# A two-layer diffusion step: the columns of shift and scale, the first value products and the first output products in another order

## The chip, the cores and the metric

The kernel runs on one core of a Trainium2 chip. The metric is the device time of one execution in microseconds (us), taken as the median of several runs. The core has five engines, each with its own queue, worked off in order: PE (TensorE, matrix products; its weight loads are listed as PEld), DVE (VectorE), ACT (ScalarE), POOL (GpSimd) and SP (SyncE, which issues most DMA transfers). ACT issues transfers too, in the same queue as its computation.

## The reference

One inference step with two layers over 512 latent tokens and 128 context tokens, 1024 channels wide. Layer 0 mixes tokens by neighbourhood attention, layer 1 by grouped attention; behind each mixer stands a gated feed-forward part (FFN) with a convolution of width 3. Before each part the tokens are normed and get a scale and a shift that are computed from a conditioning vector:

```python
sh_ap, sc_ap, g_ap, ... = adaln(c_ctx, ada_w[l], ada_b[l])      # silu(c) @ w + b, in six pieces
hs = rmsnorm(xs, norm_mix_pre[l]) * (1.0 + sc_as) + sh_as
qs, ks_, vs = na_qkv(hs, na_w_qkv[i])                            # h @ w_qkv
os_ = neighbourhood_attention(qs, ks_, vs, ...)                  # softmax over near keys and all context keys
xs = xs + g_as * rmsnorm(os_ @ w_o, norm_mix_post[l])
```

The change is within layer 0's mixer: from the first loads to the products with `w_o`.

## The kernel before, in words

A product of two fp32 matrices is made of three passes with rounded operands (`passes`, L176): high part by high part, high by low, low by high. So each weight tile of 128x1024 numbers (512 KB) is loaded as `wr`, cast by ACT to its high part `wh` (L165), and DVE or POOL subtracts to get the low part `wl` (L167, `wsplit`). The same is done for activations: `hT` is a pair of tensors with the channels on the partitions (eight blocks k = 0 to 7 of 128 channels) and the 640 tokens in the columns.

**The start** (L483 to L632). Five token tiles `x_0` to `x_4` are loaded, normed (`x_norm`) and turned by PE (`x_turn`, `tr`) into `xT`. The scale and shift of the first layer come in four groups of 256 channels each. For a group, `mod_load` loads four tiles `wf` of `ada_w`, `mod_rows` makes a `row` of 16 products, ACT copies it to `rs`, and `mod_cols` turns it by four products `col` into columns `gcol` and `hcol` for two blocks k. With these ACT makes the high part of `hT` (L568), and DVE scales `xT` (L569) and makes the low part (L570). The first 256 of 1024 value columns are then made: `v_part(i, cs)` adds, for the token tiles in `cs`, the products `vp` of the blocks 2i and 2i + 1, 15 for a block over all five tiles. These products of group i need the columns of group i and the value weights `wv`, loaded in two tiles of four blocks each.

**The heads** (from L740). Sixteen heads in eight pairs. A generator `stream` yields one step after the other of the remaining products: queries and keys of a pair (`qk`, six products a step) and values (`vp`). `fill()` runs one step. Ahead of head 0, `PRO` steps are run. For each head, `scores` of four slots make products `s`, DVE adds a bias table `tb` and finds the minimum `nm`, ACT makes exponentials `p`, POOL scales them (L918); `turns` 0 to 2 turn them by PE (`tp`), and `values` multiplies pairs of heads with the values (`po`). A list of words sets the order on PE: `ORDER` for heads 0 to 12, `ORDER2` from 13, in two variants for even and odd heads. `f` is a step of the stream, `s0` to `s3` are scores of the next head, `t0` to `t2` turns of this head, `v` the values of the last two heads. In heads 1, 5, 9 and 13, `p0` makes the context tokens' own scores (`sp`, POOL's scaling at L658), `p1` turns them (`tp<-ident,pp`), `p2` multiplies them with the values. The bias table of a head is built by POOL from three loads `tr` that ACT issues (L870), into one buffer for all heads.

When the stream has ended, the products with `w_o` (`y`, `part0(t, p)`: three products of 512 columns for token tile t and pair p) take its place: the generator `early`, started behind head 12. They need the split outputs `oh` and `ol` of the pair (`o_split`, L960 and L961) and split weights.

PE's order is fixed as written: each PE instruction is tied to the one before. On the other engines a scheduler sets the order.

Of the kernel before, what the change touches and what calls it, by code (L numbers as in the profile page):

```python
# [2 lines left out]

# [15 lines left out]
P = 128  # L19
# [82 lines left out]
def hybrid_step(ctx: ExitStack, tc: tile.TileContext, A, O):  # L102
# [16 lines left out]
    def f32(t):  # L119
        return t.bitcast(F32)  # L120
# [17 lines left out]
    nc.sync.dma_start(cc[0:8, :], A["c"].rearrange("o (k p) -> (o k) p", p=P))  # L138
    nc.sync.dma_start(cc[8:16, :], A["c_ctx"].rearrange("(k p) -> k p", p=P))
    nc.sync.dma_start(cc[16:32, :], A["ada_b"][0, 0:2048].rearrange("(k p) -> k p", p=P))  # L140
    nc.sync.dma_start(cc[32:40, :], A["norm_mix_pre"][0].rearrange("(k p) -> k p", p=P))
    nc.sync.dma_start(ident, A["k_ident"])
# [17 lines left out]
    def wsplit(src, a, b, low=None, own=None, pin=False):  # L160
# [4 lines left out]
        i = nc.scalar.copy(hi, raw)  # L165
        lo = q.tile([P, a, b], F32R, tag="wl", name="wl")
        j = (low or nc.vector).tensor_sub(lo, raw, f32(hi))  # L167
        if pin:
            tc.keep_in_program_order(i)
            tc.keep_in_program_order(j)  # L170
        return hi, lo
# [307 lines left out]
    vts_of = {}  # L479
    with ExitStack() as s:  # L480
        sp = s.enter_context(pool("st"))
        sel = sp.tile([P, 2], F32, name="sel")
        nc.vector.tensor_reduce(sel, ident.rearrange("p (j q) -> p q j", q=32)[:, 0:2, :], axis=AX.X, op=ALU.add)  # L483
# [9 lines left out]

        ct = bk.get("ct")
# [55 lines left out]
        def mod_cols(i, rs):  # L550
# [14 lines left out]
            for k in (2 * i, 2 * i + 1):  # L565
                for q, cs in ((0, slice(0, NS)), (1, slice(NS, T))):
                    g1, h1 = gcol[:, k, q : q + 1], hcol[:, k, q : q + 1]
                    nc.scalar.activation(hT[0][:, k, cs], xT[:, k, cs], AF.Identity, bias=h1, scale=g1)  # L568
                    nc.vector.tensor_scalar(xT[:, k, cs], xT[:, k, cs], g1, h1, op0=ALU.mult, op1=ALU.add)  # L569
                nc.vector.tensor_sub(hT[1][:, k, 0:T], xT[:, k, :], f32(hT[0][:, k, 0:T]))  # L570
# [4 lines left out]
        def wv_load(i):  # L575
            wv[i] = wsplit(rows(wqkv, 4 * i, 4, 2048, 256), 4, 256, nc.gpsimd)

        def x_in_norm(ts):
            for t in ts:
                x_load(t)  # L580
                x_norm(t)
# [3 lines left out]
        for i in range(2):  # L585
            loads[i + 1] = mod_load(i + 1)
            wv_load(i)
# [4 lines left out]
        def v_part(i, cs):  # L592
            for c in cs:
                for k in (2 * i, 2 * i + 1):
                    wh, wl = wv[k // 4]
                    passes(vb[c][:, 0:256], tuple(x[:, k, c * P : c * P + P] for x in hT),
                           (wh[:, k % 4, :], wl[:, k % 4, :]), k == 0, k == KC - 1)
                if i == 3:
                    na_v_put(vts_of[0], c, vb[c][:, 0:256])
                    if c == 4:  # L600
                        na_v_out(0, vb[c][:, 0:256])
                    bk.put(vb[c])
# [29 lines left out]
        v_part(3, range(NT))  # L632
# [107 lines left out]
    with l_na:  # L740
# [39 lines left out]
        def na_qk_items(p):  # L780
            d = {}

            def load_q():
                d["w"] = wsplit(rows(wqkv, 0, 8, P * p, P), 8, P, nc.gpsimd)
                kc = ap.tile([P, P], F32, tag="kc", name="kc", bufs=2)
                nc.scalar.dma_start(
                    kc, A["cache_na_k"][0, 0][:, 2 * p : 2 * p + 2, :].rearrange("t h d -> t (h d)")
                )
                d["kc"] = kc

            def load_k():
                d["wk"] = wsplit(rows(wqkv, 0, 8, 1024 + P * p, P), 8, P, nc.gpsimd)
# [209 lines left out]
        def fill(n=1):  # L1002
            for _ in range(n):
                next(work, None)
# [4 lines left out]
        for slot in range(4):  # L1009
            head.scores(slot)  # L1010
            fill()
        for h in range(H):
# [3 lines left out]
            order = (ORDER if h < 13 else ORDER2)[h % 2]  # L1016
# [32 lines left out]
            if h == 11:  # L1049
                drain(ada0)  # L1050
# [5 lines left out]
            if h == 12:  # L1056
# [10 lines left out]
                def early():  # L1067
                    for ts in (range(2), range(2, NT)):
                        for p in range(6):
                            for t in ts:  # L1070
                                m0.part0(t, p)
                                yield

                work = early()
# [784 lines left out]
```

## Time and profile before

| | us |
|---|---|
| median of 3 runs (lowest, highest) | 1602.42 (1601.96, 1604.28) |
| the profiled execution | 1601.92 |
| its span, first to last instruction | 1600.1 |
| PE busy, DVE, ACT, POOL | 1537.8, 1023.9, 859.8, 710.9 |
| mean granted clock of PE | 0.983 |

A line of the timeline reads: start and length in us, engine, line, instruction, output<-inputs, shapes, count, and in brackets the idle time of the engine before it and what ended that. A line can be that of a helper: L114 and L117 are all products and turns. Products of plain fp32 numbers (`row`, `col`, `ada`) are counted twice in the trace. A granted clock of 0.50 means that PE's products take twice as long.

### The profile page before, as it was taken

The numbers are of one execution on the slowest core, as the hardware profiler recorded it, in microseconds if no ns is written. First come the engines' busy times: TensorE is split into PE (matmuls) and PEld (weight loads), VectorE is DVE, ScalarE is ACT, GpSimd is POOL, SyncE is SP. The second block draws the span as 40 slices with busy tenths as digits, with TensorE's granted clock in tenths as the row PEclk, the third lists the DMA queues.
The fourth block names the chain that finished last, engine by engine and source line by source line (L and its number), as shares of the span: only waits on it lengthen the run. The fifth ranks groups of instructions, "written<-read, shape, count | busy, mean of one in ns | idle before, by whom it ended". The sixth has DMA issues, their size and how long they took to land.

```text
span 1600.1 us, 26043 instructions
## 1 busy us (share of the span) xinstructions
PE 1537.8 (96%) x9709; PEld 1357.3 (85%) x9709; DVE 1023.9 (64%) x1650; ACT 859.8 (54%) x1641; POOL 710.9 (44%) x609
## 2 busy tenths in 40 slices
PE   5999999899999999999999898999999999999998
PEld 3989899778999999988887676777899999998886
DVE  3453533638877666665656867773787888876454
ACT  3474655545555555554453536764656565565343
POOL 1654544423255445534444344441324655553433
PEclk8999999899999999999999998999999999999999
DMA  9745454227466566578573110003644333348664
GB/s 288 188 112 146 115 156 117 65 69 234 140 197 203 195 211 184 188 255 288 169 238 132 60 40 14 2 1 106 234 125 158 117 114 108 105 158 269 207 213 139
DMA packets 193210, 242.41 MB, mean 151 GB/s; under 512 B 11100, under 2 KB 149564, under 8 KB 193084
## 3 DMA queue, kind: packets, MB, share of 16 engines
q1 hardware_dynamic: 182224, 233.13, 45.4%
q10 hardware_dynamic: 10860, 7.62, 2.7%
q8 instruction: 76, 1.25, 0.3%
q14 instruction: 50, 0.41, 0.1%
HBM read 214.38 MB, written 26.34 MB: 150 GB/s over the span
## 4 chain that ended last, share of the span: by engine, by line
PE 55%; DVE 9%; POOL 5%; ACT 3%; issue 3%; DMA 1%; ACTq 0%; POOLq 0%; DVEq 0%
PE acc L114 18%; PE ux L114 15%; PE uz L114 6%; PE uy L114 4%; PE y L114 2%; PE s L114 2%; PE po L114 2%; PE tp L117 2%; PE ada L114 2%; POOL wl L1147 1%; DVE t L1223 1%; POOL vl L1147 1%; DVE al L1147 1%; POOL rh L1467 1%; DVE wl L167 1%
## 5 line engine op out<-in xcount | busy, mean ns | idle before, releaser
L167 POOL TENSOR_TENSOR wl<-wr,wh 128x1024 fp32r<-128x1024 f32 x74 | 183.1, 2476 | 261.7 <-ACT wh L165 252.3
L1147 POOL TENSOR_TENSOR wl<-wr,wh 128x1024 fp32r<-128x1024 f32 x76 | 183.5, 2437 | 39.5 <-ACT wh L1146 35.9
L114 PE MATMUL ux<-B,wh 128*128 128x322 f32 x832 | 199.9, 311 | 0.7 <-ACT u L1200 0.7
L1223 DVE SCALAR_TENSOR_TENSOR t<-C,cw,t 128x644 f32<-128x644 f32 x176 | 156.3, 888 | 56.0 <-ACT t L1221 55.6
L114 PE MATMUL acc<-wh,alo 128*128 128x512 f32 x440 | 172.3, 392 | 0.5 <-DVE alo L1116 0.5
L114 PE MATMUL acc<-wh,ahi 128*128 128x512 f32 x440 | 172.0, 391 | 0.0
L114 PE MATMUL acc<-wl,ahi 128*128 128x512 f32 x440 | 171.9, 391 | 0.0
L165 ACT CAST wh<-wr 128x1024 fp32r<-128x1024 f32 x140 | 145.3, 1048 | 40.7 <-DMA wr<-in_ffn_w_down 30.9
L114 PE MATMUL uz<-B,wh 128*128 128x322 f32 x640 | 156.2, 312 | 0.7 <-ACT v L1200 0.7
L114 PEld LDWEIGHTS ux<-B,wh 128*128 128x128 f32 x832 | 143.4, 189 | 3.2 <-ACT u L1200 1.0
L1116 DVE TENSOR_TENSOR alo<-ain,ahi 128x384 fp32r<-128x384 f32 (+1 forms) x88 | 80.3, 930 | 85.7 <-ACT ahi L1114 84.7
L114 PE MATMUL ux<-B,wl 128*128 128x322 f32 x416 | 129.3, 311 | 2.7 <-DVE wl L1147 2.7
L114 PE MATMUL qk<-hT,wh 128*128 128x384 f32 (+1 forms) x512 | 122.9, 317 | 0.1
L114 PEld LDWEIGHTS uz<-B,wh 128*128 128x128 f32 x640 | 111.2, 189 | 3.6 <-ACT vh L1146 1.6
L1221 ACT ACTIVATE t<-C,cw 128x644 f32<-128x644 f32 x88 | 78.6, 894 | 53.8 <-DVE C L1251 41.1
L1147 POOL TENSOR_TENSOR vl<-wr,vh 128x1024 fp32r<-128x1024 f32 x38 | 96.3, 2534 | 24.6 <-ACT vh L1146 24.3
L1146 ACT CAST wh<-wr 128x1024 fp32r<-128x1024 f32 x84 | 84.9, 1049 | 40.9 <-DVE wr L1170 40.5
L167 DVE TENSOR_TENSOR wl<-wr,wh 128x1024 fp32r<-128x1024 f32 x66 | 86.9, 1329 | 22.6 <-ACT wh L165 22.0
L114 PE MATMUL uz<-B,wl 128*128 128x322 f32 x320 | 99.5, 311 | 0.0
L114 PEld LDWEIGHTS acc<-wh,alo 128*128 128x128 f32 x440 | 82.5, 188 | 19.1 <-DVE alo L1116 1.4
L114 PEld LDWEIGHTS acc<-wl,ahi 128*128 128x128 f32 x440 | 82.6, 188 | 17.8
L114 PEld LDWEIGHTS acc<-wh,ahi 128*128 128x128 f32 x440 | 82.6, 188 | 17.8
(251 smaller groups left out, 3965.3 us busy)
## 6 DMA issues: line engine op xcount, KB each, us to landing
wr<-in_ffn_w_up SPq DMA_DIRECT2D x88, 512.0 KB
wr<-in_ffn_w_down SPq DMA_DIRECT2D x88, 512.0 KB
wr<-in_ada_w SPq DMA_DIRECT2D x80, 512.0 KB
act<-act SPq DMA_DIRECT2D x44, 321.0 KB
wr<-in_na_w_qkv SPq DMA_DIRECT2D x24, 512.0 KB
mod<-modrow SPq DMA_DIRECT2D x20, 512.0 KB
ain<-act SPq DMA_DIRECT2D x44, 192.0 KB
wf<-in_ada_w SPq DMA_DIRECT2D x16, 512.0 KB
```

Of the source, the lines that this page charges most:

```text
L114: pe(nc.tensor.matmul(*a, **k))
L117: pe(nc.tensor.transpose(*a, **k))
L165: i = nc.scalar.copy(hi, raw)
L167: j = (low or nc.vector).tensor_sub(lo, raw, f32(hi))
L1116: pin(nc.vector.tensor_sub(lo[:, 0 : c1 - c0], ain[:, 0 : c1 - c0], f32(hi[:, 0 : c1 - c0])))
L1146: nc.scalar.copy(hl[0], src)
L1147: low.tensor_sub(hl[1], src, f32(hl[0]))
L1221: nc.scalar.activation(t, taps(0), AF.Identity, bias=cw[:, 3, n : n + 1], scale=cw[:, 1, n : n + 1])
L1223: nc.vector.scalar_tensor_tensor(t, taps(d), cw[:, w, n : n + 1], t, op0=ALU.mult, op1=ALU.add)
L1467: last_rms[0] = nc.gpsimd.tensor_tensor(r, v, mhalf.broadcast_to([P, n]), op=ALU.pow)
```

## The change

- SP loads `x_0` ahead of the small constants and the identity; these follow, then the other tokens.
- The first tile of value weights is loaded between the first and the second group of `wf`.
- On PE, the columns of a group follow its rows directly, apart from the second to fourth group, where 6, 9 and 9 value products stand in between. The value products go block by block over all token tiles: `v_part(k, cs)`.
- The low parts of the value weights, and of the first pair's query and key weights, are made by DVE, not POOL. The first pair's query weights are split behind the last step of `hT`.
- One more step is run ahead of head 0 (`PRO` 20), one fewer among its scores; head 0 has a list of its own.
- `p0` stands at the front of the lists of odd heads. From head 13 the words are in another order.
- Behind the last key products, the four products `part0` of pairs 0 and 1 and token tiles 0 and 1 are part of the same generator; they come before head 13.

```diff
+ORDER0 = "f f f t0 s0 f s1 t1 f f t2 f a f f s2 s3 f f f f f".split()
 ORDER = (
     "f f t0 s0 f s1 t1 f f t2 f a f f s2 s3 f f f f f f".split(),
-    "f f p0 t0 s0 f s1 t1 f t2 p1 f f f v a p2 s2 s3 f f f".split(),
+    "p0 f f t0 s0 f s1 t1 f t2 p1 f f f v a p2 s2 s3 f f f".split(),
 )
 ORDER2 = (
-    "t0 s0 s1 f f f f t1 f f t2 f f f s2 f f s3 f f f".split(),
-    "t0 p0 s0 s1 f f f f t1 t2 p1 f f f v p2 s2 f s3 f f".split(),
+    "t0 s0 s1 f f f t1 f t2 f s2 f s3 f f f f f f f".split(),
+    "p0 s0 s1 t0 f f f t1 f t2 f s2 p1 f s3 v p2 f f f f".split(),
 )
-PRO = 19
+PRO = 20
...
+        x_load(0)
+        const_loads()
...
-            wv[i] = wsplit(rows(wqkv, 4 * i, 4, 2048, 256), 4, 256, nc.gpsimd)
+            wv[i] = wsplit(rows(wqkv, 4 * i, 4, 2048, 256), 4, 256)
...
         loads[0] = mod_load(0)
-        for i in range(2):
-            loads[i + 1] = mod_load(i + 1)
-            wv_load(i)
+        wv_load(0)
+        loads[1] = mod_load(1)
+        loads[2] = mod_load(2)
+        wv_load(1)
         loads[3] = mod_load(3)
...
         rs = mod_rows(0, loads[0])
-        for i in range(1, 3):
-            nxt = mod_rows(i, loads[i])
-            mod_cols(i - 1, rs)
-            rs = nxt
-        v_part(0, (0, 1))
+        mod_cols(0, rs)
+        rs = mod_rows(1, loads[1])
+        v_part(0, range(2))
+        mod_cols(1, rs)
+        v_part(0, range(2, NT))
+        v_part(1, range(NT))
+        rs = mod_rows(2, loads[2])
+        v_part(2, range(3))
         mod_cols(2, rs)
-        v_part(0, (2, 3, 4))
-        v_part(1, range(NT))
+        v_part(2, range(3, NT))
+        v_part(3, range(NT))
         rs = mod_rows(3, loads[3])
-        v_part(2, (0, 1, 2))
+        v_part(4, range(3))
         mod_cols(3, rs)
-        v_part(2, (3, 4))
+        v_part(4, range(3, NT))
+        v_part(5, range(NT))
...
-                d["w"] = wsplit(rows(wqkv, 0, 8, P * p, P), 8, P, nc.gpsimd)
+                d["w"] = wsplit(rows(wqkv, 0, 8, P * p, P), 8, P, nc.gpsimd if p else None, after=None if p else normed)
...
             if h == 11:
+                def early(ps, *rows_):
+                    for ts in rows_:
+                        for p in ps:
+                            for t in ts:
+                                m0.part0(t, p)
+                                yield
+
+                work = chain(work, early(range(OEARLY), range(2)))
...
-                work = early()
+                work = chain(early(range(OEARLY, 6), range(2)), early(range(6), range(2, NT)))
```

How this moves instructions is shown at three places. The first is PE at the start, where the last token tile has been turned (`tr`) and rows, columns and value products (`vp`) follow. Before:

```order
L117 MATMUL tr<-ident,x_4_189 128x128 x8
L114 MATMUL row<-wf,scolp 32x256 x32
L114 MATMUL col<-sel,rs 128x2 x4
L114 MATMUL row<-wf,scolp 32x256 x16
L114 MATMUL col<-sel,rs 128x2 x4
L114 MATMUL vp<-wh,hT_127 128x256
```

With the change:

```order
L119 MATMUL tr<-ident,x_4_189 128x128 x8
L116 MATMUL row<-wf,scolp 32x256 x16
L116 MATMUL col<-sel,rs 128x2 x4
L116 MATMUL row<-wf,scolp 32x256 x16
L116 MATMUL vp<-wh,hT_122 128x256
```

The first value product stood behind three groups of rows and two of columns; now it stands behind two of rows and one of columns.

The second place is ACT between the first value products and the first scores: casts of weights (`wh`), table loads (`tr`), queries (`qs`) and keys (`kp`, `kh`). Before, in part:

```order
L870 DMA tr<-in_k_rpb 128x1x249
L463 COPY vt<-vp 128x256
L474 COPY vo<-vp 128x256
...
L870 DMA tr<-in_k_rpb 64x1x249 x2
L824 ACTIVATE qs_668<-qk 64x256
L824 ACTIVATE qs_669<-qk 64x256
...
L870 DMA tr<-in_k_rpb 64x1x249
L797 CAST kh_741<-tk 64x128
...
L839 COPY kp<-qk 128x128
L797 CAST kh_740<-qk 64x384
```

With the change, in part:

```order
L841 ACTIVATE qs_668<-qk 64x256
L170 CAST wh<-wr 128x1024
L841 ACTIVATE qs_669<-qk 64x256
L887 DMA tr<-in_k_rpb 128x1x249
...
L887 DMA tr<-in_k_rpb 128x1x249
L887 DMA tr<-in_k_rpb 64x1x249 x2
L856 COPY kp<-qk 128x128
L814 CAST kh_740<-qk 64x384
```

The loads of the first table stood ahead of the first `qs` and now stand behind the second; those of the third table stood ahead of a part of the first `kh` and now stand right ahead of `kp`.

The third place is PE where the last key products have ended: the scores `s` of head 13, the turn of `kp`, turns `tp` of head 13's probabilities, context scores `sp`, scores of head 14, and the products `y` with `w_o`. Before:

```order
L114 MATMUL s<-kl_616,qs_2780 128x384
L117 MATMUL tk<-ident,kp 128x128
L117 MATMUL tp<-ident,p 128x128 x4
L114 MATMUL sp<-kh_2940,qs_2779 128x128
...
L114 MATMUL s<-kl_617,qs_3337 128x384
L114 MATMUL y_3676<-wh,oh_3423 128x512
```

With the change:

```order
L116 MATMUL s<-kl_616,qs_2780 128x384
L119 MATMUL tk<-ident,kp 128x128
L116 MATMUL y_3591<-wh,oh_3423 128x512
...
L116 MATMUL sp<-kh_2940,qs_2779 128x128
...
L116 MATMUL s<-kl_617,qs_3337 128x384
L119 MATMUL tp<-ident,p 128x128 x4
```

Twelve `y`, the eight `sp` and the four `s` stood behind the first four turns of head 13 and now stand ahead of them.

More of the change, by code (lines that the diff above doesn't have):

```diff
@@ L492, in x_load @@
             xts.append(xt)
+        x_load(0)
+        const_loads()
+        sel = sp.tile([P, 2], F32, name="sel")
+        nc.vector.tensor_reduce(sel, ident.rearrange("p (j q) -> p q j", q=32)[:, 0:2, :], axis=AX.X, op=ALU.add)
         ct = bk.get("ct")
@@ L631, in hybrid_step @@
             bk.put(cp)
[L632 removed]
+        v_part(6, range(NT))
+        for c in range(NT):
+            v_part(7, (c,))
+            na_v_put(vts_of[0], c, vb[c][:, 0:256])
+            if c == 4:
+                na_v_out(0, vb[c][:, 0:256])
+            bk.put(vb[c])
     def prompt_scores(ap, sides):
```

56 lines of the change are left out of this document (25 added, 31 removed).

## The prediction, made before the changed kernel ran

> **What bounds the kernel now.** I read the page first, then the busy time of stretches, then the matrix engine's timeline where the stretches show idle time.
>
> ```profile
> span 1600.1 us, 26043 instructions
> PE 1537.8 (96%) x9709; PEld 1357.3 (85%) x9709; DVE 1023.9 (64%) x1650; ACT 859.8 (54%) x1641; POOL 710.9 (44%) x609
> 0.00:40.00 40.00, 23.28 (x156) 13.65 (x157) 13.22 (x26) 15.09 (x27) 6.43 (x17) 0.83 0.98 288
> 40.00:80.00 40.00, 37.92 (x282) 36.07 (x282) 17.12 (x33) 18.93 (x37) 24.07 (x20) 0.91 0.76 188
> 300.00:400.00 100.00, 92.49 (x482) 76.31 (x480) 60.26 (x109) 53.82 (x132) 31.51 (x53) 0.95 0.42 138
> ```
>
> PE is the bound: it idles 1600.1 − 1537.8 = 62.3 us in all. A gain can only be idle PE time, or PE time at a lower clock. The stretch rows (start:end, length, busy us of PE, PEld, DVE, ACT, POOL, granted clock, DMA share, GB/s) put 16.7 us of it in the first 40, 2.1 in the next 40 and 7.5 in 300 to 400, each with a clock under 1. Outside 0 to 400 no instruction moves, save some DVE, ACT, POOL and SP rows of the first FFN. Stretches of 2 us show how long the clock stays down:
>
> ```profile
> 26.00:28.00 2.00, 1.21 (x12) 0.34 (x16) 0.00 (x0) 0.00 (x0) 0.00 (x0) 0.61 1.09 346
> 46.00:48.00 2.00, 2.00 (x15) 2.00 (x15) 2.00 (x6) 1.75 (x4) 0.34 (x1) 0.77 1.22 290
> 84.00:86.00 2.00, 2.00 (x10) 2.00 (x9) 1.72 (x5) 1.96 (x4) 2.00 (x1) 0.61 0.04 9
> 86.00:88.00 2.00, 2.00 (x8) 1.91 (x8) 0.23 (x1) 1.60 (x6) 0.94 (x2) 0.53 0.26 70
> 306.00:308.00 2.00, 0.00 (x0) 0.00 (x0) 1.69 (x7) 1.96 (x6) 1.67 (x3) 0.58 0.58 218
> 316.00:318.00 2.00, 2.00 (x10) 1.53 (x10) 0.00 (x0) 0.87 (x4) 1.04 (x1) 0.86 0.09 36
> ```
>
> The clock falls to half near 27 and is back near 47; falls near 85 and is back near 88; falls near 307 and is back at 316 to 317. Half of each PE-busy us in between is lost.
>
> The start, PE's timeline (start, length, instruction, idle before it and releaser; fp32 products without rounding count twice):
>
> ```profile
> 20.95 1.93 PE L114 MATMUL row<-wf,scolp 128*32 128x256 f32 x32
> 23.41 0.64 PE L114 MATMUL row<-wf,scolp 128*32 128x256 f32 x8 [0.53 <-DMA wf<-in_ada_w]
> 27.84 1.08 PE L114 MATMUL row<-wf,scolp 128*32 128x256 f32 x8 [0.46 <-DMA wf<-in_ada_w]
> 39.40 0.56 PE L114 MATMUL vp<-wh,hT 128*128 128x256 f32 x1
> 55.77 0.95 PE L114 MATMUL col<-sel,rs 128*128 128x2 f32 x8
> 64.60 0.28 PE L114 MATMUL qk<-hT,wh 128*128 128x256 f32 x1
> ```
>
> Who waited for `hT` between 39 and 65 us (us, times):
>
> ```profile
>   PE vp L114: 2.1, 3
> ```
>
> From 23.4 to 27.8 PE takes each tile of the second group of `ada_w` as it lands, one per (27.84 − 23.41)/3 = 1.48 us. The first value product waits until three groups of four tiles are in (39.40) though it needs columns of the first alone. So the start is bound first by transfers, until shortly before 39.4, then by PE at half clock, and at its end by DVE making `hT`.
>
> **The change, part by part.**
>
> *Start.* x_0 moves from sixth to first on SP:
>
> ```profile
> 0.72 0.40 SPq L138 DMA_DIRECT2D cc<-in_c  x1
> 2.63 2.58 SPq L489 DMA_DIRECT2D x<-in_x_sample  x4
> 7.69 1.06 ACT L511 ACTIVATE junk<-x 128x1024 bf16<-128x1024 f32 x1 [2.93 <-DMA x<-in_x_sample]
> ```
>
> x_0 is issued 1.9 us earlier; x_1 is not, since five small loads now stand between. What counts is how much sooner the saturated stream runs: 0 to 1.9 us; I take 1.3, because x_0 now uses time in which little else moved. The first tile of value weights now precedes the second group: one tile, 1.48 us. The last tile of that group reaches PE at 27.84 + 1.48 − 1.3 = 28.0, its products take 1.08, and the first value product follows at 29.1, not 39.4.
>
> Are its columns there? The first group ends at 20.95 − 1.3 + 1.93 = 21.6; the copy of its row to SBUF I put at 0.7, the column product at 0.95 (row 55.77): 23.2. Then DVE:
>
> ```profile
> 33.47 2.09 DVE L569 TENSOR_SCALAR xT<-xT,gcol,hcol 128x128 f32<-128x128 f32 x1 [0.78 <-ACT hT L568]
> 33.12 2.36 POOL L167 TENSOR_TENSOR wl<-wr,wh 128x1024 fp32r<-128x1024 f32 x1 [14.11 <-ACT wh L165]
> 56.76 0.16 DVE L561 SCALAR_TENSOR_TENSOR gcol<-col,colb 128x4 f32<-128x4 f32 x1 [2.69 <-PE col L114]
> 60.67 0.82 DVE L570 TENSOR_TENSOR hT<-xT,hT 128x640 fp32r<-128x640 f32 x1
> L167 DVE TENSOR_TENSOR wl<-wr,wh 128x1024 fp32r<-128x1024 f32 x66 | 86.9, 1329 | 22.6 <-ACT wh L165 22.0
> ```
>
> With POOL quiet both columns are done 61.49 − 56.76 = 4.7 us after the column product. The weight split moved from POOL to DVE adds 1.33, so 23.2 + 4.7 + 1.3 = 29.2 for the second column, covered, since PE needs the second column only after 15 more products and a column product, some 4 us later. The old place cost as well: beside POOL's split a 128x128 step took 2.09 us.
>
> First value product to first key/query product (39.40 to 64.60) took 25.2 us. Into it move a column product (0.95) and a row group (1.93): +2.9. Out go the three `hT` waits, 2.1, as 21 products and the `cp` turns now stand between each last column product and its use. The half clock lasted 7.4 us from 39.40; the fall near 307 lasted to 316.5, 6.2 us after PE was busy again at 310.3. I take 6.2: half of 1.2, −0.6. For new waits (`cr`, fourth row group) I add 0.5. Sum 25.2 + 2.9 − 2.1 − 0.6 + 0.5 = 25.9, first key/query product at 55.0: **9.6 us gained** (7 with no head start and one late tile, 12.5 at best).
>
> [...]
>
> *First scores.* ACT carries the bias table loads in its queue:
>
> ```profile
> 66.14 1.45 ACTq L870 DMA_DIRECT2D tr<-in_k_rpb  x2
> 68.53 0.38 ACT L824 ACTIVATE qs<-qk 64x256 fp32r<-64x256 f32 x1 [0.48 <-DVE qs L825]
> 77.37 1.21 ACTq L870 DMA_DIRECT2D tr<-in_k_rpb  x2
> 82.64 0.44 PE L114 MATMUL s<-kh,qs 128*128 128x384 f32 x1 [1.46 <-ACT kh L798]
> ```
>
> The first table's loads now follow the second `qs` (68.53): 2.4 us later against the products. One buffer serves all tables, so the third table's loads, behind which stand `kp` and the last `kh`, come later too and hold ACT. One more step of six products stands before the scores; at half of the width of a `y` product (0.25 us, below) these are 0.7. I take +2.4 − 0.7 − 0.8, a third of the delay, as slack: **0.9 lost** (1.7 gained if the wait goes, 2.4 lost if nothing hides it).
>
> *Prompt scores* go two steps ahead in heads 1, 5 and 9:
>
> ```profile
>   PE tp L117: 1.3, 3
> ```
>
> This row of the view of tile `pp` (who waited for it; us, times; 80 to 260 us) counts the three waits of PE's turns for POOL's scaled probabilities. Two steps of six products now stand in between, which is longer than 1.3/3 = 0.4 us, so they should go: **1.2 gained**. The bounds are 1.3 and 0; 0 if POOL, not PE's order, sets when `pp` is ready.
>
> *End of the key products.*
>
> ```profile
> 300.31 2.40 POOL L167 TENSOR_TENSOR wl<-wr,wh 128x1024 fp32r<-128x1024 f32 x1
> 304.38 0.38 PE L117 MATMUL tp<-ident,p 128*128 128x128 f32 x2
> 309.16 0.47 PE L117 MATMUL tp<-ident,p 128*128 128x128 f32 x1 [4.40 <-POOL p L918]
> 310.29 0.48 PE L117 MATMUL tp<-ident,p 128*128 128x128 f32 x1 [0.65 <-POOL p L918]
> 317.72 1.04 PE L117 MATMUL tp<-ident,p 128*128 128x128 f32 x8
> 318.95 0.48 PE L114 MATMUL y<-wh,oh 128*128 128x512 f32 x1
> 321.21 2.81 PE L114 MATMUL po<-pk,vt 128*64 128x512 f32 x20
> 329.25 0.33 PE L117 MATMUL tp<-ident,p 128*128 128x128 f32 x1 [1.15 <-POOL p L918]
> ```
>
> The turn waits for the last probabilities, ready at 310.3. Now 12 `y`, 8 `sp` and 4 `s` stand before it. Nine `y` took 321.21 − 318.95 = 2.3, so 12 take 3.0; `sp` and `s`, narrower, I put at 1.7 by their widths: PE runs from 304.4 to 309.1, still waits for the last one, and at 310.7 stands where it stood at 317.7: 7.0. The `y` need weights that POOL finished at 302.7. The 1.15 at 329.25 ends behind 12 `y`. In the last pair the turns stand right before the value products: −0.3. **7.9 gained** (4 if the `y` wait for splits, 8.2 at most).
>
> Sum: 9.6 − 0.9 + 1.2 + 7.9 = 17.8. The profiled execution took 1601.92 (span 1600.1), which gives 1584.1; the median of the runs stands 0.5 above it: **1584.6 us**.
>
> **The rivals.**
>
> *The start stays bound by transfers or DVE.* For it: DMA share 1.09 at 26 to 28. Against: the later groups are no longer needed at once. If the third group lands three tiles late (4.4), and DVE's steps meet POOL once (1.8), the start gains 3.4: 1590.8.
>
> *The first output products wait.* Splits of `oh`, `ol` and weights come from ACT and DVE, which are busy when PE idles (1.96 and 1.69 of 2 us at 306). Against: the first are done by 302.7. If PE idles 4 us and the clock falls, 2 of 7.9 remain: 1590.5.
>
> *The clock comes back sooner.* The fall at 85 lasted only 3 us. At the start that saves half of 6.2 − 3: 1583.0.
>
> *Slower: the first FFN.* Its rows on SP, ACT and DVE come in another order, and PE waits there already:
>
> ```profile
> 400.42 0.41 PE L114 MATMUL ux<-B,wl 128*128 128x322 f32 x1 [1.40 <-DVE wl L1147]
> ```
>
> If that wait came in each of 22 blocks, 31 us would be lost: 1615. It decides from 17.8/22 = 0.8 us per block. Against: the order differs in the first blocks only. That the change does nothing is excluded by PE's new order, except where each gain is eaten: 1602.
>
> **How the numbers follow.** Forecast 0.71 (own range 1580 to 1589), start bound 0.11, output products 0.08, clock 0.05, FFN 0.03, nothing 0.02. Within 0.2%, 3.2 us, a measurement of this kernel can't tell a change. Faster is the first four, 0.95, of which I leave 0.01 to the middle: faster 0.94, same 0.03, slower 0.03. The best bounds of the terms together (12.5 + 1.7 + 1.3 + 8.2 = 23.7) give 1578.7, the worst (7 − 2.4 + 0 + 4 = 8.6) 1593.8, which needs all four at once. The range is 1578.5 to 1593, which takes in the first two rivals and leaves out FFN, nothing and the far ends of the bounds.
>
> **What would show it.** The first `vp` near 29 and the first `qk` near 55, no wait on `hT` over 0.5; the wait at the first `s` at 1.5 to 4; no wait at `tp<-ident,pp`; the granted clock at 1 through what was 300 to 330, and a wait of 1 to 2 us at the first turn of head 13. Wrong it would be if `vp` starts after 33, if `y` waits on `wl`, or if waits appear beyond 400.

## The result: 1585.2 us, 1.1% faster

The changed kernel takes 1585.22 us (median of 4 runs, 1584.86 to 1585.74), the kernel before 1603.1 us beside it. The ratio is 0.9889, with a 95% interval of 0.9872 to 0.9906. The time forecast was 1584.6 us. The sum is right; one of its four terms is wrong by 5 us, and smaller errors of the other sign make up for it. One execution of the kernel with extra turns (below) took 6550.16 us and is left out of its numbers.

The page of the changed kernel, and the busy time of the stretches shown of before (start:end, length, busy us of PE, PEld, DVE, ACT, POOL, granted clock, DMA share, GB/s):

```profile
span 1583.0 us, 26047 instructions
PE 1525.7 (96%) x9709; PEld 1351.9 (85%) x9709; DVE 1022.9 (65%) x1654; ACT 862.1 (54%) x1641; POOL 700.9 (44%) x605
0.00:40.00 40.00, 25.96 (x194) 19.27 (x195) 15.43 (x33) 18.23 (x32) 4.42 (x16) 0.87 1.02 301
40.00:80.00 40.00, 32.60 (x262) 30.85 (x261) 15.15 (x34) 19.63 (x41) 16.05 (x18) 0.92 0.76 192
300.00:400.00 100.00, 97.88 (x552) 83.24 (x551) 70.94 (x116) 56.41 (x129) 30.34 (x51) 1.00 0.42 138
```

PE's idle time falls only from 62.3 to 57.3 us. The other 12.1 us are busy time: the same count of products takes so much less, in part because fewer of them run at half clock (the mean granted clock is 0.988, for 0.983). The first and the third stretch have more PE time and a higher clock than before; the second holds 5.3 us less PE time than before.

PE's timeline at the start (start, length, instruction, idle before it and releaser):

```profile
19.71 1.93 PE L116 MATMUL row<-wf,scolp 128*32 128x256 f32 x32
27.74 1.08 PE L116 MATMUL row<-wf,scolp 128*32 128x256 f32 x8 [0.45 <-DMA wf<-in_ada_w]
28.75 0.58 PE L116 MATMUL vp<-wh,hT 128*128 128x256 f32 x1
54.14 0.28 PE L116 MATMUL qk<-hT,wh 128*128 128x256 f32 x1
```

The first value product follows the second row group at once, at 28.75 in place of 39.40, and the first query product comes at 54.14 in place of 64.60. The gain up to here is 10.46 us. Then PE's row at the first scores, ACT's rows ahead of it (ACTq are the transfers that ACT issues), and stretches of 2 us:

```profile
78.85 0.69 PE L116 MATMUL s<-kh,qs 128*128 128x384 f32 x1 [7.40 <-ACT kh L815]
```

```profile
58.54 0.38 ACT L841 ACTIVATE qs<-qk 64x256 fp32r<-64x256 f32 x1
60.73 2.04 ACTq L887 DMA_DIRECT2D tr<-in_k_rpb  x3
63.32 0.48 ACT L841 ACTIVATE qs<-qk 64x384 fp32r<-64x384 f32 x1 [4.39 <-DMA tr<-in_k_rpb]
69.32 1.24 ACTq L887 DMA_DIRECT2D tr<-in_k_rpb  x2
70.61 0.22 ACT L841 ACTIVATE qs<-qk 64x64 fp32r<-64x64 f32 x1 [5.36 <-issue]
75.80 1.84 ACTq L887 DMA_DIRECT2D tr<-in_k_rpb  x3
77.68 0.27 ACT L856 COPY kp<-qk 128x128 f32<-128x128 f32 x1 [3.23 <-issue]
```

```profile
36.00:38.00 2.00, 2.00 (x30) 1.44 (x33) 0.41 (x1) 0.00 (x0) 0.00 (x0) 0.90 1.09 348
76.00:78.00 2.00, 0.00 (x0) 0.00 (x0) 0.00 (x0) 0.32 (x2) 0.00 (x0) 0.50 0.42 36
84.00:86.00 2.00, 2.00 (x12) 2.00 (x11) 0.99 (x3) 0.87 (x3) 0.69 (x2) 0.95 0.85 251
```

PE waits 7.40 us for keys, where it waited 1.46 before. ACT casts them, and ACT stands three times, 4.39, 5.36 and 3.23 us, with `tr` loads at the head of its queue (waiting to go out, and going out). In the wait the clock falls, and the scores of head 0 run at half clock until some 84.2: the granted clock is 0.50 in each stretch of 2 us from 78 to 84, and a `qk` product of 384 columns starts 0.32 us behind the one ahead (79.92 to 80.24), for 0.18 at full clock (84.78 to 84.96), so 1.8 times as long rather than twice. The last stretch, where the key products end:

```profile
304.18 0.33 PE L119 MATMUL tp<-ident,p 128*128 128x128 f32 x1 [0.87 <-POOL p L935]
384.98 0.41 PE L116 MATMUL ux<-B,wl 128*128 128x322 f32 x1 [1.18 <-DVE wl L1165]
```

Of the waits of 4.40, 0.65 and 1.15 us on POOL's `p`, 0.87 is left, and the granted clock is 1.00 throughout.

Points that both kernels pass, on PE's timeline (us), give the ledger. Two of them before, and the same two with the change:

```profile
98.02 1.07 PE L114 MATMUL ada<-wr,scolp 128*32 128x256 f32 x16
299.52 0.63 PE L117 MATMUL tp<-ident,p 128*128 128x128 f32 x4 [0.89 <-DVE qs L825]
```

```profile
94.67 1.07 PE L116 MATMUL ada<-wr,scolp 128*32 128x256 f32 x16
293.27 0.63 PE L119 MATMUL tp<-ident,p 128*128 128x128 f32 x4 [0.90 <-DVE qs L842]
```

| point | before | after | gained up to here | of it since the point above |
|---|---|---|---|---|
| first `qk` | 64.60 | 54.14 | 10.46 | 10.46 |
| first `ada`, behind the first scores | 98.02 | 94.67 | 3.35 | −7.11 |
| first wait of head 12, end of it | 299.52 | 293.27 | 6.25 | 2.90 |
| first FFN wait, end of it | 400.42 | 384.98 | 15.44 | 9.19 |
| end of the span | 1600.1 | 1583.0 | 17.1 | 1.7 |

### The profile page after: what moved, and what is told of

It is laid out like the page before. It is cut to its first block, busy times and chain, and to the rows that moved or that the text cites. A ratio compares the mean times of both kernels' runs of the same rounds, so it can differ in the third digit from the quotient of the medians.

```text
span 1583.0 us, 26047 instructions
## 1 busy us (share of the span) xinstructions
PE 1525.7 (96%) x9709; PEld 1351.9 (85%) x9709; DVE 1022.9 (65%) x1654; ACT 862.1 (54%) x1641; POOL 700.9 (44%) x605
## 4 chain that ended last, share of the span: by engine, by line
PE 57%; DVE 9%; POOL 5%; issue 3%; ACT 3%; DMA 1%; ACTq 0%; POOLq 0%; DVEq 0%
PE acc L116 18%; PE ux L116 16%; PE uz L116 7%; PE uy L116 4%; PE y L116 2%; PE s L116 2%; PE po L116 2%; PE tp L119 2%; PE ada L116 2%; POOL wl L1165 1%; POOL vl L1165 1%; DVE t L1241 1%; POOL rh L1485 1%; DVE al L1165 1%; DVE wl L172 1%
## 5 line engine op out<-in xcount | busy, mean ns | idle before, releaser
L172 POOL TENSOR_TENSOR wl<-wr,wh 128x1024 fp32r<-128x1024 f32 x70 | 172.6, 2467 | 235.7 <-ACT wh L170 235.4
L1165 POOL TENSOR_TENSOR wl<-wr,wh 128x1024 fp32r<-128x1024 f32 x76 | 183.6, 2438 | 45.8 <-ACT wh L1164 42.0
```

Source lines behind the costliest of these rows:

```text
L1165: low.tensor_sub(hl[1], src, f32(hl[0]))
```

## The experiments

My theory for the wrong term is that ACT, in order, is held by table loads that wait, and that the keys stand behind them. The rivals were that the loads land late whatever holds them, that the casts set the wait, and that the extra step ahead of the scores does. All ratios below are to the kernel before, with 95% intervals.

### A second buffer for the table loads

```diff
-            tr = ap.tile([P, 2, RUN], F32, tag="tr", name="tr", bufs=1)
+            tr = ap.tile([P, 2, RUN], F32, tag="pk" if h == 1 else "tr", name="tr", bufs=NPK if h == 1 else 1)
```

> The changed kernel with a second buffer for the table loads: head 1's `tr` takes a slot of the `pk` ring, which is idle until the first turns. PE's order is unchanged. Theory A (the 7.40 us wait at the first `s` is ACT held behind the loads of head 1's and head 2's tables, which wait for one buffer): ACT casts `qs` and `kh` without the holds of 5.36 and 3.23 us, the wait falls to 1 to 2.5 us, the granted clock doesn't fall between 74 and 84, and the time falls by the 5 to 6 us of the wait and some 2.5 us of half clock: 1576 to 1580.5. Theory B (the loads themselves land late, 3.4 to 5 us after their issue, whatever buffer they have, and POOL's tables or the casts behind them stay late): the wait stays at 5 to 7.5 us and the time at 1584 to 1586.

Measured: 1582.38 us, 0.9872 (0.9857 to 0.9887). That is between the two: 2.8 us gained on the changed kernel. PE's wait and ACT's rows:

```profile
75.69 0.69 PE L116 MATMUL s<-kh,qs 128*128 128x384 f32 x1 [3.77 <-ACT kh L815]
```

```profile
61.41 4.03 ACTq L887 DMA_DIRECT2D tr<-in_k_rpb  x6
65.48 0.48 ACT L841 ACTIVATE qs<-qk 64x384 fp32r<-64x384 f32 x1 [6.09 <-DMA tr<-in_k_rpb]
71.51 0.22 ACT L841 ACTIVATE qs<-qk 64x64 fp32r<-64x64 f32 x1 [4.09 <-issue]
```

The buffer is only a part of the hold. Six loads now go out in a row, and issuing them alone takes ACT's queue 4.03 us; the third table's loads still wait. The wait halves, as ACT's holds shrink from 13.0 to 10.2 us.

### Nineteen steps ahead of the scores, as before

```diff
-PRO = 20
+PRO = 19
-            fill(slot < 3)
+            fill()
-            order = (ORDER if h < 13 else ORDER2)[h % 2] if h else ORDER0
+            order = (ORDER if h < 13 else ORDER2)[h % 2]
```

> The changed kernel with 19 steps ahead of the first scores, as before, and head 0's old order. Theory A (ACT's hold sets when the first `s` can run): the step is no longer cover, so the wait grows by the step's 0.7 us to some 8 us, the step is done later and the time is the same within 1 us: 1584.5 to 1586.5. Theory B (the extra step itself makes the keys late, by another result to copy ahead of them): the wait falls under 4 us and the time by 3 us or more.

Measured: 1585.18 us, 0.9895 (0.988 to 0.991), the same as the changed kernel. The extra step isn't the cause. (The profiled execution took 1589.42, 4.2 above the median; its wait of 9.84 us at the first `s` is therefore not a fair size, but theory B asked for less than 4.) From the first `ada` (96.11) to the first wait of head 12 (295.83) this kernel takes 199.72 us, the changed one 198.60 (six kernels here with this order and the table loads in their place, the changed one among them, take 198.57 to 198.79). So about 1.1 us of the 7.11 lost at the scores is work done early that heads 1 to 12 need not do: the true loss is 6.0.

### Tables of heads 1 and 2 behind the keys

```diff
-                    nc.scalar.copy(d["kh"][b][oth, c0:c1], src[own])
+                    khs[p] = nc.scalar.copy(d["kh"][b][oth, c0:c1], src[own])
...
-                nc.scalar.dma_start(dst, ...)
+                i = nc.scalar.dma_start(dst, ...)
+                if h in (1, 2):
+                    behind(i, khs[0])
```

> The changed kernel with the table loads of heads 1 and 2 ordered on ACT behind the last cast of `kh` of heads 0 and 1; still one buffer, the same loads, the same PE order. Theory A (ACT is held by loads that wait: for the one buffer, 5.36 and 3.23 us in the changed kernel; with a second buffer still 6.09 and 4.09 us, in part for the six issues themselves at 0.6 to 0.67 us each and for earlier transfers, and the wait at the first `s` fell only from 7.40 to 3.77 us): with the loads behind the casts only the first hold of 4.4 us stays, which ends at 63.3, the wait falls under 1.5 us, the clock stays up, and the time falls by 8 to 11 us, to 1574 to 1577. Theory B (the casts themselves and the first table set the wait; the loads only fill time in which ACT waits for products): the wait stays at 3 to 7 us and the time at 1581 to 1585.

Measured: 1582.98 us (1580.56 to 1585.47), 0.9874 (0.9858 to 0.9891). The four executions fall in two pairs, 1580.56 and 1580.79, 1585.16 and 1585.47, and the profiled one is the longest. By the time and by the wait that is left (3.44 us) theory B holds, but the timeline says more:

```profile
73.25 0.47 PE L116 MATMUL s<-kh,qs 128*128 128x384 f32 x1 [3.44 <-ACT kh L815]
110.46 4.50 PE L116 MATMUL po<-pk,vt 128*64 128x512 f32 x20 [1.96 <-DVE qs L842]
```

```profile
94.56 0.27 ACT L856 COPY kp<-qk 128x128 f32<-128x128 f32 x1 [5.50 <-issue]
```

The first `ada` comes at 88.34, 6.3 us sooner than in the changed kernel. Then ACT is held 5.5 us at the same loads later on, in front of the next pair's `kp`, PE waits twice for what depends on it (1.80 us at 98.65, 1.96 at 110.46), and the value products run at half clock (4.50 in place of 2.81). By head 12 only 0.3 us are left. In this execution the hold was moved, not removed; what the shorter pair did, no trace shows. Of the 3.44 us left at the first `s`, ACT's hold of 5.2 us by the first table is one cause and a copy that waits 4.0 us for a cache load (`vc`) another; this kernel doesn't tell the two apart.

### Table loads on SP

```diff
-                nc.scalar.dma_start(dst, raw_ap(A["k_rpb"], ...))
+                nc.sync.dma_start(dst, raw_ap(A["k_rpb"], ...))
```

> The changed kernel with all table loads on SP in place of ACT. Theory A (ACT is held by the loads): ACT has no hold any more, the first `s` waits under 1.5 us; but SP now waits for the one buffer, and the weight loads behind it come later, which costs up to 3 us in some later step: 1574 to 1580. Theory B (the first table or the casts set the wait): the wait stays over 3 us, 1581 to 1587.

Measured: 1575.18 us (1573.65 to 1577.98), 0.9828 (0.9813 to 0.9842): 10.0 us faster than the changed kernel. PE at the first `qk`, at the first scores, which now wait for nothing, and up to the first `ada`:

```profile
52.33 0.28 PE L116 MATMUL qk<-hT,wh 128*128 128x256 f32 x1
69.47 0.34 PE L116 MATMUL s<-kh,qs 128*128 128x384 f32 x1
78.09 0.33 PE L119 MATMUL tp<-ident,p 128*128 128x128 f32 x1 [1.04 <-POOL p L935]
84.14 1.07 PE L116 MATMUL ada<-wr,scolp 128*32 128x256 f32 x16
```

The first `ada` comes at 84.14 in place of 94.67. Of these 10.5 us, 1.8 come ahead of the first `qk` (52.33 for 54.14), where no product needs the tables: the first value products of this execution ran at full clock, those of the changed kernel at half. From the first `qk` to the first `ada` PE takes 31.81 us in place of 40.53, so the hold is worth 8.7 us there. ACT's holds by loads of tables are gone, the wait of 7.40 us is gone, and the granted clock is 1.00 in each stretch of 2 us from 70 to 100. Theory A holds: what stood between the earlier products and the gain was the table loads in ACT's queue. The move to SP does two things that this run doesn't tell apart: it takes the loads out of a queue that also computes, and it lets the first of them go out at 47.20 in place of 60.73.

### The kernel before with table loads on SP

```diff
-                nc.scalar.dma_start(dst, raw_ap(A["k_rpb"], ...))
+                nc.sync.dma_start(dst, raw_ap(A["k_rpb"], ...))
```

> The kernel before with all table loads on SP in place of ACT, and nothing else. Theory A (in the kernel before ACT's hold costs only what its trace shows at the first scores, 1.7 us of waits and half of some 4 us at half clock from 84 to 88; the change made the hold costly): 1.5 to 4 us faster than before, 1599 to 1601, with the wait of 1.46 us at the first `s` gone. The changed kernel with the loads on SP then stands 23 to 26 us below it, not 17.9. Theory B (the move to SP is worth the same 10 us in either kernel and has nothing to do with the change): 1591 to 1595.

Measured: 1595.62 us, 0.9954 (0.9941 to 0.9966), 7.5 us faster than before. Neither range holds it:

```profile
81.01 0.34 PE L114 MATMUL s<-kh,qs 128*128 128x384 f32 x1
302.46 0.47 PE L117 MATMUL tp<-ident,p 128*128 128x128 f32 x1 [3.02 <-POOL p L918]
```

At the first `ada` 3.7 us are gained (94.29 in place of 98.02), which is theory A's size. Another 2.8 come from the last heads to the first FFN wait, where the wait of 0.89 us on `qs` is gone and that on POOL's `p` is 3.02 in place of 4.40 and 0.65. That second place I had not thought of. From the first `qk` to the first `ada` the old kernel takes 33.42 us, and 29.69 with the loads on SP. So the hold cost 3.7 us there in the old kernel and 8.7 in the changed one: the change made it 5.0 us dearer. By the kernel that follows, in which PE does not wait for POOL's `p` and takes 30.40 us, it is 10.1 and 6.4. The loss of 6.0 in the ledger lies between. Without the hold the change is worth 1595.6 − 1575.2 = 20.4 us, not 17.9.

### Table loads on SP, and two buffers

```diff
-            tr = ap.tile([P, 2, RUN], F32, tag="tr", name="tr", bufs=1)
+            tr = ap.tile([P, 2, RUN], F32, tag="pk" if h % 2 and h < 2 else "tr", name="tr", bufs=NPK if h % 2 and h < 2 else 1)
...
-                nc.scalar.dma_start(dst, raw_ap(A["k_rpb"], ...))
+                nc.sync.dma_start(dst, raw_ap(A["k_rpb"], ...))
```

> The changed kernel with the table loads on SP and a second buffer for head 1's. Theory A (with the loads on SP the one buffer holds SP, not ACT, and what stands behind them on SP is needed late enough): the same within 1 us as with one buffer, 1574 to 1577. Theory B (SP's hold at 58 to 69 delays weights or the tables, which shows in the waits of 1.04 us on POOL's `p` near 78): 1572 to 1574.

Measured: 1572.49 us (1572.13 to 1573.89), 0.9809 (0.9796 to 0.9823), the fastest of all; theory B, by its time. The wait of 1.04 us on `p` near 78 is gone and the first `ada` comes at 83.23. POOL now makes five of the six steps of the first two tables in a row, 57.15 to 61.35. This is 12.7 us faster than the changed kernel. Of the 2.7 us between the medians of one and two buffers the traces show 0.9, at the first `ada`; the two profiled executions took 1573.65 and 1573.89 us, so the rest is not shown.

### The end of the key products, undone and alone

Undone, in the changed kernel (the old `ORDER2` with it):

```diff
-                work = chain(work, early(range(OEARLY), range(2)))
...
-                work = chain(early(range(OEARLY, 6), range(2)), early(range(6), range(2, NT)))
+                work = early()
```

> The changed kernel with the old order of the last heads and the old place of the first output products (start, first scores and prompt scores as changed). Theory A (the parts are independent; the end of the key products is worth the 9.2 us that the two traces show between the first turn of head 12 and the first FFN wait): 1594.4, within 1 us, with the wait of some 4.4 us on POOL's `p` back and the clock low for 8 to 10 us near 300. Theory B (the parts share a gain, the end being worth only what was forecast, 7.9, or less, since the start has already moved it): 1590 to 1593.

Alone, in the kernel before (the new `ORDER2` with it):

```diff
+                work = chain(work, early(range(OEARLY), range(2)))
...
-                work = early()
+                work = chain(early(range(OEARLY, 6), range(2)), early(range(6), range(2, NT)))
```

> The kernel before with the new order of the last heads and the first output products in their new place, and nothing else. Theory A (independent parts): 9.2 us faster than before, 1593 to 1595. Theory B (the gain there needs the earlier start): 3 us or less, above 1599.

Measured: 1593.34 us without it, 0.9937 (0.9921 to 0.9954); 1594.33 us with it alone, 0.9947 (0.9932 to 0.9962). It is worth 8.1 us in the one comparison and 9.1 in the other, beside 9.19 in the ledger. The two parts are nearly independent: the early part alone gives 1603.47 − 1593.34 = 10.1 us and the late part alone 9.1, 19.2 in all, and together they give 17.9.

### The constants first again

```diff
-        x_load(0)
         const_loads()
+        x_load(0)
```

> The changed kernel with the five small constant loads issued ahead of x_0, as before. Theory A (the head start of x_0 is worth the 1.23 us by which the turn of the last tile and the first row group came sooner): the first row group and the first `vp` (28.75) come 1.0 to 1.9 us later, and the time, at a start bound by transfers until the last tile of the second group lands, is 1586 to 1587.5. Theory B (the stream that counts is the one behind x_4, which starts when the five small loads are through, either way): the first `vp` moves by less than 0.5 us and the time by less than 0.5.

Measured: 1588.4 us, 0.9905 (0.9888 to 0.9921), 3.2 us slower than the changed kernel. PE's first row group and first value product:

```profile
20.76 1.93 PE L116 MATMUL row<-wf,scolp 128*32 128x256 f32 x32
30.26 0.58 PE L116 MATMUL vp<-wh,hT 128*128 128x256 f32 x1
```

They come 1.05 and 1.51 us later, as theory A has it, and the first `ada` 1.48 later; the time is 0.9 us over its range. The row group alone doesn't tell: in the nine kernels here that load `x_0` first and have no extra turns it starts between 19.18 and 21.67. But their first `vp` stands between 28.42 and 29.42, so this one is 0.8 to 1.8 us later than all of them. So the head start of `x_0` is real: the forecast had 1.3. The other 1.7 us of the median are in no place that the edit touches: from the first FFN wait to a wait in layer 1, the same instructions in the same order, 558.5 us stand against 556.8 (more on this below).

### Low parts of the value weights on POOL again

```diff
-            wv[i] = wsplit(rows(wqkv, 4 * i, 4, 2048, 256), 4, 256)
+            wv[i] = wsplit(rows(wqkv, 4 * i, 4, 2048, 256), 4, 256, nc.gpsimd)
```

> The changed kernel with the low half of the two tiles of value weights made on POOL again. Theory A (POOL's split slows the DVE steps beside it: before, a 128x128 step took 2.09 us beside one): the DVE steps of the first or second `hT` group get longer by 1.5 us and more each, a wait of 1 to 3 us at `vp` on `hT` or `wl` comes up, and the first `qk` (54.14) comes 1 to 3 us later: 1586 to 1588. Theory B (21 products and a row group now stand between the columns and their use): no wait on `hT`, the same within 0.5 us, or up to 0.5 us faster as DVE is relieved of 2.6 us.

Measured: 1585.45 us, 0.989 (0.9875 to 0.9904): the same. DVE beside POOL's split:

```profile
24.99 0.15 DVE L573 TENSOR_TENSOR hcol<-col,colb 128x4 f32<-128x4 f32 x1
25.11 2.06 DVE L572 TENSOR_TENSOR gcol<-gcol,colb 128x4 f32<-128x4 f32 x1
24.79 2.36 POOL L172 TENSOR_TENSOR wl<-wr,wh 128x1024 fp32r<-128x1024 f32 x1 [6.68 <-ACT wh L170]
```

Both theories saw one half. A DVE step of four columns, 0.16 us elsewhere, takes 2.06 beside the split and ends with it (27.17 and 27.15); beside the second split it takes 1.84. But DVE is spared 1.22 us of its own, and PE shows a single wait of 0.62 us on `hT`. Where the split is made doesn't matter here.

### Turns in the waits of the start

```diff
+        def warm(n):
+            for _ in range(n):
+                turn(vb[4][:, 0:P], ident, ident)
...
+            if i == 0:
+                warm(5)
...
+                if i == 1 and (n, h) != (1, 1):
+                    warm(5)
```

> The changed kernel with 20 more turns of `ident` on PE in the waits of the start: five ahead of the first column products and five behind each of the first three tiles of the second group of `ada_w`, into a bank that the value products overwrite later. They leave nothing out and change no result. Theory A (the clock falls near 26.5 since PE is idle for more than half of 24 to 28; with PE busy through these waits it stays up): the granted clock stays at 1 from 26 to 36, the 8.7 us of products at half clock shrink by 4.3, the first `qk` comes 3 to 4.3 us sooner than 54.14, and, as ACT's hold at the first `s` follows the key and query products, the time falls by 1 to 4 us: 1581 to 1584. Theory B (the clock falls whatever PE does there, or the transfers set the first `qk`): the clock falls as before and the time is 1585 to 1587, the extra turns costing up to 1.5 us.

Measured: 1585.42 us (three executions, 1584.90 to 1586.52), 0.9892 (0.9876 to 0.9907): the time of theory B. But the clock looks as theory A has it:

```profile
20.00:22.00 2.00, 2.00 (x18) 1.21 (x20) 0.69 (x1) 0.59 (x1) 0.00 (x0) 0.50 1.09 348
26.00:28.00 2.00, 2.00 (x22) 1.21 (x18) 1.84 (x3) 1.93 (x4) 0.00 (x0) 1.00 1.10 349
```

It is at 1.00 from 24 to 70. In this execution it had been low earlier, around 20, so turns and rows took longer (1.90 and 2.72 us), the extra turns cost some too, and the first `qk` came at 52.30, 1.8 sooner. That the turns kept the clock up is not shown: the kernel with the late part undone and the one with the loads on SP have the same start without these turns, and they too are at 1.00 from 24 to 40, with the first `qk` at 52.62 and 52.33. What is gained up to the first FFN wait (382.84 for 384.98) is lost again behind it: both spans are 1583.0. What the run shows is that the extra turns don't shorten this kernel.

### The prompt scores in their old place

```diff
-    "p0 f f t0 s0 f s1 t1 f t2 p1 f f f v a p2 s2 s3 f f f".split(),
+    "f f p0 t0 s0 f s1 t1 f t2 p1 f f f v a p2 s2 s3 f f f".split(),
```

> The changed kernel with the prompt score products of heads 1, 5 and 9 back in their old place, two steps later; all else as changed. Theory A (the term as forecast: three waits of 0.41 to 0.45 us at the prompt turns come back, and the three new ones of 0.24 to 0.27 us at `po` on `qs` go): from the first `ada` to the first wait of head 12 PE takes 0.5 us more than the 198.60 of the changed kernel, 199.1, and the time is 1585.5 to 1586. Theory B (the 2.9 us that these heads gained, 201.50 against 198.60, come from the prompt products alone): 201 to 201.5 there, 1587.5 to 1588.5. What then is left to the step done ahead of the first scores is 2.4 us by A and nothing by B.

Measured: 1587.34 us, 0.9905 (0.9888 to 0.9921). From the first `ada` to the first wait of head 12 it takes 94.13 to 294.22, 200.09 us: 1.5 more than the changed kernel, between the theories. The first of the three waits, and what it replaces in the changed kernel:

```profile
109.46 0.66 PE L119 MATMUL tp<-ident,pp 128*128 128x128 f32 x4 [0.45 <-POOL pp L675]
```

```profile
112.50 2.81 PE L116 MATMUL po<-pk,vt 128*64 128x512 f32 x20 [0.27 <-DVE qs L842]
```

From the first `ada` to the end of that wait at `po` PE takes 17.83 us in the changed kernel, the new wait included, and 18.33 to the same `po` with the old place: 0.5 us in each of three heads. The idle times in brackets give less, 1.31 us of old waits and 0.75 of new ones, since a wait cost more than its idle time here: in a row of products each starts before the listed end of the one ahead (in the changed kernel the `qk` at 54.14 is listed with 0.28 us, and the next starts at 54.25), and behind a wait it doesn't. From the turns `tp` ahead of the old wait to the product behind it takes 1.46 us (108.41 to 109.87), and 0.79 without a wait in the changed kernel (108.96 to 109.75): 0.67 us for 0.45 of idle time. The prompt products are worth 1.5 us and the early step 1.1, together 2.6 of the 2.9 that heads 1 to 12 gained; 0.3 is not accounted for.

## Why the prediction was right, and where it was wrong

*Start, 9.6 us forecast: 10.5 measured, right.* The first `vp` came at 28.75 for 29.1, the head start was 0.8 to 1.8 for 1.3, and the waits on `hT` are gone. Two pieces were off and cancel in part: the half clock lasted 7.6 us behind the first `vp`, not 6.2, and the 0.5 for new waits didn't come. Some 0.7 us of the stretch went faster than my sum, because the waits on `hT` had cost more than the 2.1 us of idle time that I took out. Before, around the last of the three:

```profile
60.18 0.28 PE L114 MATMUL vp<-wl,hT 128*128 128x256 f32 x1
61.54 0.50 PE L114 MATMUL vp<-wh,hT 128*128 128x256 f32 x2 [1.08 <-DVE hT L570]
61.88 0.28 PE L114 MATMUL vp<-wl,hT 128*128 128x256 f32 x1
```

From one `wl` product to the next takes 1.70 us here, 1.08 and 1.16 at the other two waits (53.39 to 54.47, 59.02 to 60.18), and 0.35 where PE does not wait: together the three cost 2.9. The size of the start differs between executions, too: in the kernels here with this start and no extra turns the first `qk` came between 52.33 and 54.61, which is 12.3 to 10.0 us of gain.

*First scores, 0.9 us lost forecast: 6.0 lost, wrong, and the bound of 2.4 with it.* The step that failed is "2.4 us later against the products", with its price that a third of it is slack. I had the mechanism, loads that hold ACT, and shifted one of them by its place in the order, as if it would go out as soon as its turn came. The table was not 2.4 but 8.4 us later: it was done 15.15 us after the first `qk` (69.29), against 6.77 before (71.37). POOL's rows after the change, its row before, and two stretches of 2 us after the change show what I left out:

```profile
66.21 1.70 POOL L892 TENSOR_TENSOR tb<-mask,tr 128x256 f32<-128x256 f32 x2 [5.22 <-DMA tr<-in_k_rpb]
68.42 0.87 POOL L892 TENSOR_TENSOR tb<-mask,tr 128x256 f32<-128x256 f32 x1 [0.50 <-DMA tr<-in_k_rpb]
74.92 0.85 POOL L892 TENSOR_TENSOR tb<-mask,tr 128x256 f32<-128x256 f32 x1 [0.51 <-DVE kl L816]
```

```profile
68.85 2.52 POOL L875 TENSOR_TENSOR tb<-mask,tr 128x256 f32<-128x256 f32 x3
```

```profile
58.00:60.00 2.00, 2.00 (x13) 2.00 (x12) 0.46 (x2) 0.90 (x2) 1.89 (x3) 1.00 1.00 291
60.00:62.00 2.00, 2.00 (x15) 2.00 (x15) 0.00 (x0) 0.00 (x0) 0.99 (x1) 1.00 0.11 31
```

ACT was through with the second `qs` at 58.92, and the load went out only at 60.73. Its buffer was free (on SP the load went out at 47.20). The DMA engines were full until 60 (share 1.00) and nearly idle then (0.11), so it went out when the earlier transfers had ended. That it waited for one of them is my inference; the trace names no releaser. Then 3.4 us pass to POOL's first step, in which the next weights move (DMA share 0.81 and 0.94 in the two stretches from 62 to 66), where it was no more than 1.3 us before (the last load was out at 67.6 and POOL began at 68.85, straight behind other work). And each delay counts again with the second and third table, since all share one buffer: their loads went out at 69.32 and 75.80, 0.03 us after POOL's last step on the table ahead (69.29 and 75.77). ACT stood 13.0 us, not 7.4. Finally I priced the wait without the clock: after 7.4 us of idle PE, 5.3 us ran at half clock. In the kernel with the loads on SP the casts and the extra step are the same, and PE doesn't wait at the first scores, so these were not in the way.

*Prompt scores, 1.2 forecast: 1.5.* The three waits went, as forecast. The size is over the top of its bounds by 0.2: I counted the waits by their idle time, 0.4 us each, where the first cost 0.67, and left out the new waits on `qs`.

*End of the key products, 7.9 forecast: 9.2 in the ledger, 8.1 and 9.1 by leaving it out and alone.* The mechanism is right: the products took the place of the wait and the clock stayed up. The size was off by the wait that is left, 0.87 for the 1 to 2 I gave it, and by bounds that should have had a full removal of the wait in them.

*Nothing behind 400 us forecast: 1.7 measured.* From the first FFN wait to a wait in layer 1 it took 558.08 us before (400.42 to 958.50) and 556.80 after (384.98 to 941.78), without a change in PE's order. In the experiments this stretch took between 556.7 and 559.0 us. So a difference of this size comes up between kernels that have the same instructions here, and I don't put it to the change.

Of the rivals, the start bound by transfers, the output products that wait, the clock that comes back sooner and the FFN did not come in the profiled execution.

The terms together: 5.1 us too few were lost at the scores, and 4.5 too few gained elsewhere (0.9, 0.3, 1.3 and 1.7, and the 0.3 in heads 1 to 12 that no run accounts for). So 17.8 − 0.6 = 17.2 us is left, which is the 17.1 by which the two profiled executions differ. That the forecast met the time to 0.6 us is luck: these errors cancel, and the 1.7 us behind 400 are not the change's.

## What to carry to other kernels

When products are moved ahead, walk the queue of every engine that feeds them, and ask of each transfer that it issues what it waits for at its new time: a buffer (here the second and third table's loads, out at 69.32 and 75.80), or, as I infer for the first, an earlier transfer in a full DMA (share 1.00 until 60). The loads that waited held ACT, and all that stood behind them in its queue, for 13.0 us here; moving them to a queue without computation was worth 10 us. Price an idle stretch of the matrix engine together with the half clock that follows (here 5.3 us behind 7.4). And price a short wait by the starts of the products around it: the idle time listed was about two thirds of the cost here (2.1 of 2.9 us, 0.45 of 0.67).

## What the runs showed of the hardware that I had not expected

Where the clock falls differs between executions of the same instructions. In the changed kernel the last two token tiles were turned fast (1.07 and 1.06 us, where the three ahead took 1.94 to 2.15) and the first value products ran at half clock (granted 0.50 from 28 to 36). In the kernel with two buffers and loads on SP, which has the same PE order, it was the other way round, by the times of its rows:

```profile
17.77 3.65 PE L119 MATMUL tr<-ident,x 128*128 128x128 f32 x16 [1.53 <-DVE x L523]
28.83 0.39 PE L116 MATMUL vp<-wh,hT 128*128 128x256 f32 x1
```

Sixteen turns took 3.65 us, where two times eight took 2.13 (1.07 and 1.06) in the changed kernel, and the first `vp` took 0.39 for 0.58. The first `qk` came at 52.83 for 54.14. Layer 1 has the same: in the changed kernel sixteen products `gp` at 902.09 took 5.55 us, in the kernel with the constants first, at 904.39, 4.06. Within one kernel, too, the mean granted clock differs: it was 0.986 to 0.991 in the four executions with the second buffer and the loads on ACT, whose times agree within 0.7 us. What makes the clock fall at one place or the other, no run here shows. One profile of such a stretch is one draw of it: with this start the first `qk` came between 52.33 and 54.61, and 1 to 2 us of a difference there are not to be explained by an edit.

A small step of one engine lasted until a large one of another ended: the DVE step of 2.06 us beside POOL's split of 2.36 us ended 0.02 us after it, while the same step takes 0.16 where no split runs beside it (at 31.59). The step just ahead of it ran beside the same split in 0.15; it reads `col`, which PE wrote, and `colb`, where the slow one reads `gcol` and `colb`. Why the one is held and the other not, no run here shows.

Six loads of 62 and 125 KB cost ACT 4.03 us of issue, 0.67 us each, more than a cast of 64x384 (0.48).
